# Linear memory in two blocks of 256 tokens, its decay factors made ahead and kept in DRAM, head outputs normed on ScalarE

## The chip, the core and the metric

One core of a Trainium2 chip runs the whole program. The time is the device time of one execution, in microseconds (us), as the median of several runs; beside it stands one profiled execution, whose own trace every duration below is taken from. The engines are TensorE (PE, with its weight loads PEld), VectorE (DVE), ScalarE (ACT), GpSimd (POOL) and SyncE (SP, which here only issues transfers). [...]

## What is computed

One layer of a streaming encoder on 512 prompt tokens and 64 sample tokens, D_MODEL = 1024: a feed-forward block, then a mixer of two branches (a linear memory with 4 heads of width 256, and a banded attention with 16 heads), then a second feed-forward block. The change touches the linear memory. For one head, with chunks of 64 tokens, the reference does

```
bcum = jnp.cumsum(lf, axis=-1)
dmat = jnp.where(causal, bcum[..., :, None] - bcum[..., None, :] + li[..., None, :], -jnp.inf)
m_t = jnp.maximum(inter, jnp.max(dmat, axis=-1))
s = jnp.einsum('bhtd,bhsd->bhts', q, k) * jnp.exp(dmat - m_t[..., None])
num = w_inter[..., None] * jnp.einsum('bhtd,bhde->bhte', q, C) + jnp.einsum('bhts,bhse->bhte', s, v)
den = w_inter * jnp.einsum('bhtd,bhd->bht', q, n) + jnp.sum(s, axis=-1)
h = num / jnp.maximum(jnp.abs(den), jnp.exp(-m_t))[..., None]
C_new = decay[..., None, None] * C + jnp.einsum('bhs,bhsd,bhse->bhde', w_s, k, v)
```

and then a layer norm of h over the head, a learned gain, a sigmoid gate from `ml_o`, and a projection. q and k come from a causal convolution of four taps with silu. The result does not depend on how the tokens are cut into chunks, so a kernel may choose its own.

## The kernel before

**Arithmetic.** Every matrix product is done in three float32r products: each operand x is split into a rounded half `hi` and the rest `lo = x - hi`, and `mm3` (line 138) issues hi*hi, hi*lo, lo*hi into one PSUM bank. A split costs one ACT instruction (the copy to `hi`) and one DVE subtraction (the `lo`), or for some weights a second ACT instruction and a transfer that adds (`add_lo`, line 222). `gemm` (line 381) makes a column tile of 128 outputs for all 576 tokens in two halves of 256 and 320 tokens, with 24 matmuls each.

**Order.** The order of PE is that of the Python program. `Order` (line 42) keeps an estimated clock `od.now`; `mm` (line 132) moves it forward by an estimate of each matmul. `later(dt, fn)` queues a function to be called dt nanoseconds of that clock later, between the steps of a `gemm`; so small products of one head lie inside the column tiles of the next. `od.bg` holds generators (`gate_rows`, `os_split`, `ht_split`) of which one step is taken at fixed distances. The order on ACT, DVE, POOL and SP is made by the tile scheduler, from priorities. PSUM has four banks with the tag "mm" and four with "aux"; `bank()` (line 123) hands out the latter.

**Gate rows.** `gate_rows` (line 1391) makes, for the four heads together, the running maximum `mrow` and rows of factors, and turns them into columns `tcol` (line 1363, 12 wide) and a split row tile `mr`.

**Attention and what follows it.** After the attention heads, a loop (line 1810) makes the gate columns 64 to 69 (`gemm` with `keep_cb`, line 1806) and `g58`; meanwhile `os_split` (line 1829) splits the eight attention outputs (names `o`, halves `os`), forms four sums of each pair in place on DVE, and splits these. Then `ap_pair` (line 1879) does the attention's projection two columns at a time in seven products of half size (`seven`, line 888) instead of eight; each product is 12 matmuls of 288 columns. Its first product takes the first splits of the outputs 4 to 7, the second those of 0 to 3, the third the second splits of 0 to 3, and the fourth the second splits of 4 to 7.

**The heads.** `ml_kq(h)` (line 1986) runs four column tiles (k in two halves, q in two halves), each followed by the convolution: ACT copies PSUM to `R`, DVE makes `U` in one and three instructions, ACT applies silu, ACT and DVE split. `turn5` (line 1973) transposes k and v into token order. `ml_decay` (line 2035) multiplies a row of `mr` by a selecting column to spread the running maximum over all partitions (`Mb`), and `decays` makes for the blocks b = 0 to 3 of 128 tokens the factors exp(a_s - M_t) for s in the block and all t from its start to 511 (widths 512, 384, 256, 128) and for the sample tokens (64 x 64); POOL blanks the part above the diagonal. `ml_early` (line 2074): `weights(b)` multiplies k and q of that shape (6 matmuls of width 512, 384, 256, 128 or 64), DVE multiplies by the factors, ACT and DVE split into `W`. `ml_late` (line 2113): `state(e)` sums the four prompt blocks into the new memory (12 matmuls) and the sample's block (3), `hidden(b)` sums over the blocks up to b (3 matmuls for each), ACT copies it to `hf`, DVE takes mean and variance; `norm` (line 2158) joins denominators and variance and does the subtraction and scaling of the five blocks on DVE; `back(e)` transposes to features and multiplies by gain and gate. The factors take exp, the convolution silu: an `order` table makes ACT do each head's exps together, with a table load (`ACT_TABLE_LOAD`) on either side.

Of the kernel before, what the change touches and what calls it, by code (L numbers as in the profile page):

```python
# [17 lines left out]
P = 128  # L18
NP_ = 512
# [67 lines left out]
def tile_layer(ctx: ExitStack, tc: tile.TileContext, ins, outs):  # L87
# [1275 lines left out]
    tcol = gp.tile([P, 5, 12], F32, name="tcol")  # L1363
# [18 lines left out]
    gdone = []  # L1382
    vf0, kf0, qf0 = (slot(F32, tp, t) for t in ("vf0", "kf0", "qf0"))
# [7 lines left out]
    def gate_rows():  # L1391
# [26 lines left out]
        for i, (a, b) in enumerate(((0, NP_), (NP_, T))):  # L1418
            ts(scol[:, 4 + i:5 + i], mrow[:, b - 1:b], -1.0, None, ALU.mult)
            yield act(rows[32:36, a:b], arow[:, a:b], AF.Exp, bias=scol[:, 4 + i:5 + i])  # L1420
# [9 lines left out]
        for b in range(5):  # L1430
            w = min(P, T - b * P)
            ps = bank()
            transpose(ps[:w, :P], rows[:, b * P:b * P + w], ident)
            yield DVE.tensor_copy(tcol[:w, b, :].rearrange("p (g h) -> p g h", h=4),
                                  ps[:w, :96].rearrange("p (g r) -> p g r", r=32)[:, :, 0:4])
# [370 lines left out]
    def keep_cb(hf, ps, j):  # L1806

        act(hs(sg[j], hf), ps, AF.Copy if j <= 3 else AF.Sigmoid)

    for j in range(KT):  # L1810
# [6 lines left out]
        if j == 3:  # L1817
# [3 lines left out]
            tstack.close()  # L1821
            ospool = tc.tile_pool(name="os", bufs=32, reuse_waits="tile")
# [6 lines left out]
            def os_split():  # L1829
# [29 lines left out]
                for s_ in sg[:4]:  # L1859
                    yield act(s_, s_, AF.Sigmoid)  # L1860
# [9 lines left out]
    def g58_cb(hf, ps):  # L1870
        act(hs(g58, hf), ps, AF.Sigmoid)
        if hf == 1:
            SP.dma_start(GD[2], g58)

    gemm(one(("in", 58)), H, [g58_cb])
    od.force(lambda: osq)
# [32 lines left out]
    ostack.close()  # L1909

# [41 lines left out]
    def conv_rest(ct, scale, room, tail=None):  # L1952
# [6 lines left out]
        with tc.issue_after(order["exp"].ins) if "exp" in order else nullcontext():  # L1959
            for a, b, u in ((0, NP_, 0), (NP_, T, NP_ + 3)):  # L1960
                order["silu"] = act(q[:, a:b], U[:, u:u + b - a], AF.Silu)
# [22 lines left out]
    hid, states, backs, order = [0], [0], [0], {}  # L1984

    def ml_kq(h):
# [19 lines left out]
        for e in range(2):  # L2006
# [9 lines left out]
            def v_turn(vf, sink):  # L2016

                if hid[0] < 5 * h:
                    later(300, lambda: v_turn(vf, sink))
                else:  # L2020
                    turn5(vf, sink)
# [13 lines left out]
    def ml_decay(h, st):  # L2035

        mb, mb2 = bank(), bank()
        pick = sel[:, h:h + 1].to_broadcast([P, P])
        mm(mb, pick, mr[:, :NP_], True, True)
        mm(mb2[:, 0:130], pick, mr[:, NP_:], True, True)  # L2040
        Mb = mp.tile([P, T], F32, tag="Mb", name=nm("Mb"))
        wdb = mp.tile([P, 66], F32, tag="wdb", name=nm("wdb"))
        with tc.high_priority(offset=120):
            act(Mb[:, :NP_], mb)
            act(Mb[:, NP_:], mb2[:, 0:64])
            act(wdb, mb2[:, 64:130])
# [8 lines left out]
        D = st["D"] = {}  # L2055

        def decays():

            for b in (4, 0, 1, 2, 3):
                s0 = b * P  # L2060
                n, w = (NP_ - s0, P) if b < 4 else (NS, NS)
                d = D[b] = mp.tile([P, n], F32, tag=f"D{b}", name=nm("D"))
                with tc.issue_after(order["silu"].ins):
                    order["exp"] = act(d[:w, :], Mb[:w, s0:s0 + n], AF.Exp, scale=-1.0, bias=tcol[:w, b, h:h + 1])

                POOL.affine_select(out=d[:w, 0:w], in_=d[:w, 0:w], pattern=[[1, w]], compare_op=ALU.is_ge, fill=0.0,
                                   base=0, channel_multiplier=-1)
            with tc.issue_after(order["exp"].ins):
                act(ch, c0v)
            tt(cl, c0v, f(ch), ALU.subtract)  # L2070

        later(6000, decays)

    def ml_early(h, st):
# [15 lines left out]
        def weights(b):  # L2090
            s0 = b * P
            n, w = (NP_ - s0, P) if b < 4 else (NS, NS)
            ps, d = bank(), D[b]
# [15 lines left out]
        for b in range(5):  # L2109

            later(10000 + 2100 * b if h == 3 else 11000 + 2600 * b, lambda b=b: weights(b))

    def ml_late(h, st):
        W, (c0, ch, cl), wdb, qs_ = st["W"], st["C"], st["wdb"], st["qs"]
        mv = mp.tile([P, 5, 2], F32, tag="mv", name=nm("mv"))
        dn = mp.tile([P, 5, 2], F32, tag="dn", name=nm("dn"))

        def state(e):
# [3 lines left out]
            for s in range(4):  # L2122
                mm3(ps[:, :258], kwh[:, s, ce], kwl[:, s, ce], vh[:, s, :], vl[:, s, :], s == 0, s == 3)
            cn = mp.tile([P, 258], F32, tag="cn", name=nm("cn"), bufs=2)
            with tc.high_priority(offset=100):
                act(cn, ps[:, :258])
            SP.dma_start(outs["pC"][h, :, e, :], cn)
            ps = bank()
            mm3(ps[:, :258], kwh[:, 4, ce], kwl[:, 4, ce], vh[:, 4, :], vl[:, 4, :], True, True)
            cn = mp.tile([P, 258], F32, tag="cs", name=nm("cs"), bufs=2)  # L2130
# [3 lines left out]
            states[0] += 1  # L2134

        def hidden(b):
# [13 lines left out]
            with tc.high_priority(offset=60):  # L2150
                act(hf_[:w, b, :], ps[:w, :258])
# [6 lines left out]
        def norm():  # L2158
# [11 lines left out]
            tt(rs, rs, r, ALU.mult)  # L2170
            for b in range(5):
                w = P if b < 4 else NS
                ts(hf_[:w, b, 0:256], hf_[:w, b, 0:256], mv[:w, b, 0:1], rs[:w, b:b + 1], ALU.subtract, ALU.mult)
# [19 lines left out]
        for e in range(2):  # L2193
            later(5500 + 1800 * e, lambda e=e: state(e))
        for b in range(5):
            later(16000 + 1800 * b if h == 3 else 19500 + 2200 * b, lambda b=b: hidden(b))
# [171 lines left out]
```

## Time and profile before

| | us |
|---|---|
| median of 3 runs (1545.62 to 1550.26) | 1546.3 |
| the profiled execution | 1547.03 |
| its span in the trace | 1544.8 |
| PE busy | 1528.6 |
| DVE busy | 1170.6 |
| ACT busy | 880.9 |
| POOL busy | 197.2 |

The profiled execution lies 0.7 us above the median, and 2.2 us of it lie outside the span. Stages in the span's time: first feed-forward and norm to about 400 us, the gate columns to about 560, attention to about 776, gate columns 64 to 69 and 58 from there to 802, the attention's projection to 847, the four heads of the linear memory to 1034, its projection, the output projection and the second feed-forward to the end.

How to read the rows: a timeline row gives start, duration, engine, line, operation, the written tile and the tiles it reads, their shape, a count, and in brackets how long the engine was idle before and what ended that. A row that groups instructions gives a count, the time in which at least one of them ran, and the mean duration. Matmuls overlap, so the time from one start to the next is the price of one, not its duration; instructions of ACT and DVE overlap by about 0.1 us when they follow each other.

### The profile page before, as it was taken

Reading aid. Unit: us, or ns where it says so; the run is one execution under the profiler, and the core shown is the slowest. Engines: PE = TensorE matmul, PEld = TensorE weight load, DVE = VectorE, ACT = ScalarE, POOL = GpSimd, SP = SyncE. Lnnn points to the kernel's source line nnn. Section 1 sums busy time; section 2 is a strip of 40 time slices with the busy share of each in tenths; the row PEclk is TensorE's granted clock in tenths of the full one; section 3 lists DMA queues with packets and bytes.
Section 4 is the critical chain, followed back from the end, with each engine's and each line's share of the span. In section 5 each row is a group of like instructions: output and inputs, shape, how many; then the busy total and the mean of one; then the engine's idle time right before and its main releaser. Section 6 shows DMA issues by size and latency. Waiting matters only on the chain.

```text
span 1544.8 us, 29439 instructions
## 1 busy us (share of the span) xinstructions
PE 1528.6 (99%) x11563; PEld 1513.4 (98%) x11563; DVE 1170.6 (76%) x2222; ACT 880.9 (57%) x1684; POOL 197.2 (13%) x370
## 2 busy tenths in 40 slices
PE   9999999999999999999999999999999999999998
PEld 9999999999999999999999999999999999999997
DVE  7877778776898767887677577775788888787765
ACT  7545446534666557777864877753456454557332
POOL 1000000100200015544200321102120000001000
PEclk9999999999999999999999999999999999999999
DMA  8322223524544449687544965542653223217333
GB/s 246 109 104 89 96 96 102 144 81 142 150 145 148 145 176 234 151 212 165 140 108 154 275 152 131 130 132 83 202 121 104 109 83 110 83 66 188 88 110 113
DMA packets 81075, 209.23 MB, mean 135 GB/s; under 512 B 9385, under 2 KB 23081, under 8 KB 80937
## 3 DMA queue, kind: packets, MB, share of 16 engines
q1 hardware_dynamic: 64936, 168.36, 32.2%
q0 software_dynamic: 14848, 37.30, 13.5%
q8 instruction: 90, 1.47, 0.4%
q10 hardware_dynamic: 1152, 1.70, 0.3%
q14 instruction: 49, 0.39, 0.1%
HBM read 170.89 MB, written 22.22 MB: 125 GB/s over the span
## 4 chain that ended last, share of the span: by engine, by line
PE 79%; DVE 9%; ACT 5%; DMA 3%; issue 3%; POOL 1%; SPq 0%; ACTq 0%; DVEq 0%; POOLq 0%
PE mm L133 67%; PE aux L133 11%; PE aux L143 1%; DVE wl L150 1%; ACT wh L147 1%; DMA s<-in_xT 1%; DVE s L150 1%; DVE sc L1608 1%; DVE s L153 1%; DVE o L150 1%; DVE U L153 1%; ACT sc L147 1%; DVE sc L157 1%; DMA wr<-in_w_in 1%; DVE kl L150 1%
## 5 line engine op out<-in xcount | busy, mean ns | idle before, releaser
L133 PE MATMUL mm<-s,wh 128*128 128x288 f32 (+2 forms) x3494 | 713.4, 298 | 1.0 <-DVE s L150 0.7
L133 PEld LDWEIGHTS mm<-s,wh 128*128 128x128 f32 x3494 | 558.7, 189 | 3.8 <-issue 0.9
L133 PE MATMUL mm<-s,wl 128*128 128x288 f32 (+2 forms) x1737 | 512.7, 295 | 0.0
L133 PEld LDWEIGHTS mm<-s,wl 128*128 128x128 f32 x1737 | 327.1, 188 | 0.2 <-DVE wl L150 0.2
L147 ACT ACTIVATE wh<-wr 128x1024 fp32r<-128x1024 f32 (+2 forms) x126 | 116.8, 935 | 108.3 <-PE mm L133 59.8
L133 PE MATMUL mm<-tx,wh 128*128 128x288 f32 x778 | 158.4, 296 | 0.0
L133 PEld LDWEIGHTS mm<-tx,wh 128*128 128x128 f32 x778 | 124.9, 188 | 0.0
L150 DVE TENSOR_TENSOR wl<-wr,wh 128x1024 fp32r<-128x1024 f32 (+2 forms) x87 | 90.8, 1053 | 36.6 <-ACT wh L147 36.5
L133 PE MATMUL mm<-tx,wl 128*128 128x288 f32 x383 | 113.0, 295 | 0.7 <-DVE wl L150 0.7
L976 ACT ACTIVATE wh<-wt 128x1024 fp32r<-128x1024 f32 x53 | 56.2, 1060 | 88.9 <-DVE wt L150 88.9
L150 DVE TENSOR_TENSOR wl<-wt,wh 128x1024 fp32r<-128x1024 f32 x53 | 64.8, 1222 | 52.6 <-ACT wh L976 52.6
L150 DVE TENSOR_TENSOR wl<-wu,wh 128x1024 fp32r<-128x1024 f32 x50 | 61.2, 1223 | 21.6 <-ACT wh L976 21.6
L223 POOL DMA_DIRECT2D s<-s x16 | 13.7, 855 | 495.0 <-ACT s L147 252.1
L133 PEld LDWEIGHTS mm<-tx,wl 128*128 128x128 f32 x383 | 72.0, 188 | 0.9 <-DVE wl L150 0.9
L147 ACT ACTIVATE h<-h 128x288 f32<-128x288 f32 x80 | 34.9, 437 | 65.2 <-DVE h L150 65.1
L976 ACT ACTIVATE wh<-wu 128x1024 fp32r<-128x1024 f32 x50 | 52.9, 1058 | 32.7 <-PE mm L133 32.5
L150 DVE TENSOR_TENSOR wl<-ws,wh 128x1024 fp32r<-128x1024 f32 x53 | 64.6, 1219 | 0.1
L150 DVE TENSOR_TENSOR ws<-wu 128x1024 f32<-128x1024 f32 x53 | 64.5, 1216 | 0.0
L133 PE MATMUL mm<-h,wh 128*128 128x256 f32 (+2 forms) x296 | 60.2, 294 | 0.0
L976 ACT ACTIVATE ah<-wu 128x512 fp32r<-128x512 f32 x53 | 33.4, 631 | 44.4 <-PE mm L133 41.3
L976 ACT ACTIVATE wh<-ws 128x1024 fp32r<-128x1024 f32 x53 | 55.8, 1052 | 0.7 <-PE mm L133 0.4
L147 ACT ACTIVATE sc<-sc,mx 128x128 f32<-128x128 f32 (+4 forms) x72 | 40.3, 560 | 25.1 <-DVE mx L1608 24.7
(420 smaller groups left out, 3609.0 us busy)
## 6 DMA issues: line engine op xcount, KB each, us to landing
wu<-in_w_gu SPq DMA_DIRECT2D x80, 512.0 KB, 4.4
wr<-in_w_in SPq DMA_DIRECT2D x46, 512.0 KB, 4.1
wl<-in_w_in POOLq DMA_DIRECT2D x38, 512.0 KB, 6.5
wr<-in_w_dn SPq DMA_DIRECT2D x34, 512.0 KB, 3.5
wu<-in_w_in SPq DMA_DIRECT2D x26, 512.0 KB, 4.7
wr<-in_w_dn SPq DMA_DIRECT2D x18, 384.0 KB, 3.5
s<-s POOLq DMA_DIRECT2D x16, 288.0 KB, 3.8
wr<-in_w_ap SPq DMA_DIRECT2D x8, 512.0 KB, 3.5
```

Source lines behind the costliest of these rows:

```text
L133: PE.matmul(out, lhsT, rhs, start=start, stop=stop, **kw)
L143: PE.transpose(out, in_, idn)
L147: return ACT.activation(out, in_, func, **kw)
L150: return (eng or DVE).tensor_tensor(out, a, b, op=op)
L153: return DVE.scalar_tensor_tensor(out=out, in0=a, scalar=s, in1=b, op0=op0, op1=op1)
L157: return (eng or DVE).tensor_scalar(out=out, in0=a, scalar1=s1, scalar2=s2, op0=op0, **kw)
L223: return POOL.dma_start(lo, src, accum_op=ALU.add)
L976: self.last = ACT.activation(hi, src, AF.Copy)
L1608: DVE.tensor_tensor_reduce(out=out, in0=ps, in1=g, op0=ALU.add, op1=ALU.min, scale=-1.0, scalar=3e38, accum_out=acc)
```

## The change

**Two blocks of 256 tokens (NC = 256).** The prompt's 512 tokens are cut in two. Within each half all is as before, so `weights(b)` has the widths 256, 128, 256, 128 and 64. `first(e)` sums blocks 0 and 1 into the memory after the first half (`cf`, split into `cfh`, `cfl`); `carried(b)` multiplies the q of blocks 2 and 3 by it, ACT scales it by a per-token factor (new columns of `tcol`, made by one more exp in `gate_rows`), and `hidden(2)` and `hidden(3)` add it on DVE instead of being copied by ACT. `second(e)` sums blocks 2 and 3 and joins them with `cf` by a factor `g`; `sample(e)` is the sample's part of what was `state`.

**Decay factors ahead.** `decay_rows(h)` makes all factors of head h and the factor g; the four heads are queued 300 + 2600 h ns after the attention's last use of its pool, in the loop of the gate columns. They go to DRAM (`DK`), and `ml_decay` fetches them into one tile with two buffers. What stays in `ml_decay` is one matmul of 66 columns. Sigmoids between the attention and the projection are held until the fourth head's exps are done (`issue_after(dexp[3].ins)`); the gate columns 64 to 69 are first copied and later passed through sigmoid.

**Norm on ScalarE.** The last step of `norm` is an `Identity` activation with scale and bias per token.

**Distances.** The `later` distances of weights, state, hidden and carried are changed, and two turns of v are kept 2500 ns apart.

Its core:

```diff
-    tcol = gp.tile([P, 5, 12], F32, name="tcol")
+    tcol = gp.tile([P, 5, 16], F32, name="tcol")
...
+    NC = NP_ // 2
...
+        yield act(rows[96:100, NC:NP_], mrow[:, NC:NP_], AF.Exp, bias=mrow[:, NC - 1:NC], scale=-1.0)
+        for i, (a, b) in enumerate(((0, NC), (NC, NP_), (NP_, T))):
...
-        act(hs(sg[j], hf), ps, AF.Copy if j <= 3 else AF.Sigmoid)
+        act(hs(sg[j], hf), ps)
...
+    def decay_rows(h):
+        mb, mb2 = bank(), bank()
+        pick = sel[:, h:h + 1].to_broadcast([P, P])
+        mm(mb, pick, mr[:, :NP_], True, True)
+        mm(mb2[:, 0:NS], pick, mr[:, NP_:T], True, True)
+        Mb = dkp.tile([P, T], F32, tag="Mb", name=nm("Mb"))
+        with tc.high_priority(offset=120):
+            act(Mb[:, :NP_], mb)
+            act(Mb[:, NP_:], mb2[:, 0:NS])
+        D = dkp.tile([P, DW], F32, tag="D", name=nm("D"), bufs=2)
+        for b in range(5):
+            s0 = b * P
+            n, w = (NC - s0 % NC, P) if b < 4 else (NS, NS)
+            d = D[:w, DB[b]:DB[b] + n]
+            act(d, Mb[:w, s0:s0 + n], AF.Exp, scale=-1.0, bias=tcol[:w, b, h:h + 1])
+            POOL.affine_select(out=d[:, 0:w], in_=d[:, 0:w], pattern=[[1, w]], compare_op=ALU.is_ge, fill=0.0,
+                               base=0, channel_multiplier=-1)
+        dexp.append(act(D[:, DG:DG + 1], Mb[:, NP_ - 1:NP_], AF.Exp, scale=-1.0, bias=Mb[:, NC - 1:NC]))
+        SP.dma_start(DK[h][:, 0:DG + 1], D[:, 0:DG + 1])
+        SP.dma_start(DK[h][0:NS, DB[4]:], D[0:NS, DB[4]:])
...
+            for h in range(4):
+                later(300 + 2600 * h, lambda h=h: decay_rows(h))
...
+                    with tc.issue_after(dexp[3].ins):
+                        yield act(s_, s_, AF.Sigmoid)
...
+    for s in sg[4:6]:
+        with tc.issue_after(dexp[3].ins):
+            act(s, s, AF.Sigmoid)
...
-            for b in (4, 0, 1, 2, 3):
-                s0 = b * P
-                n, w = (NP_ - s0, P) if b < 4 else (NS, NS)
-                d = D[b] = mp.tile([P, n], F32, tag=f"D{b}", name=nm("D"))
-                with tc.issue_after(order["silu"].ins):
-                    order["exp"] = act(d[:w, :], Mb[:w, s0:s0 + n], AF.Exp, scale=-1.0, bias=tcol[:w, b, h:h + 1])
+        D = st["D"] = mp.tile([P, DW], F32, tag="D", name=nm("D"), bufs=2)
+        SP.dma_start(D[:, 0:DG + 1], DK[h][:, 0:DG + 1])
+        SP.dma_start(D[0:NS, DB[4]:], DK[h][0:NS, DB[4]:])
...
-            for s in range(4):
-                mm3(ps[:, :258], kwh[:, s, ce], kwl[:, s, ce], vh[:, s, :], vl[:, s, :], s == 0, s == 3)
+            for s in range(2):
+                mm3(ps[:, :258], kwh[:, s, ce], kwl[:, s, ce], vh[:, s, :], vl[:, s, :], s == 0, s == 1)
+            with tc.high_priority(offset=100):
+                act(cf[:, e, :], ps[:, :258])
+            act(cfh[:, e, :], cf[:, e, :])
+            tt(cfl[:, e, :], cf[:, e, :], f(cfh[:, e, :]), ALU.subtract)
...
+                stt(cn, cf[:, e, :], st["g"][:, 0:1], ps[:, :258], ALU.mult, ALU.add)
...
+        def carried(b):
+            ps = bank()
+            for e in range(2):
+                qh, ql = (x[:, b * P:(b + 1) * P] for x in st["q"][e])
+                mm3(ps[:, :258], qh, ql, cfh[:, e, :], cfl[:, e, :], e == 0, e == 1)
+            with tc.high_priority(offset=100):
+                act(hc_[:, b - 2, :], ps[:, :258], scale=tcol[:, b, 12 + h:13 + h])
...
-                          vh[:, s, :], vl[:, s, :]) for s in range(b + 1)]
+                          vh[:, s, :], vl[:, s, :]) for s in range(b // 2 * 2, b + 1)]
...
+                if b in (2, 3):
+                    tt(hf_[:, b, :], ps[:, :258], hc_[:, b - 2, :], ALU.add)
...
-                ts(hf_[:w, b, 0:256], hf_[:w, b, 0:256], mv[:w, b, 0:1], rs[:w, b:b + 1], ALU.subtract, ALU.mult)
+                act(hf_[:w, b, 0:256], hf_[:w, b, 0:256], AF.Identity, bias=dn[:w, b, 1:2], scale=rs[:w, b:b + 1])
...
-            later(16000 + 1800 * b if h == 3 else 19500 + 2200 * b, lambda b=b: hidden(b))
+            later(17000 + 1800 * b if h == 3 else 20500 + 2200 * b, lambda b=b: hidden(b))
```

More of the change, by code (lines that the diff above doesn't have):

```diff
@@ L1958, in conv_rest @@
         hi, lo = room(), room()
-        with tc.issue_after(order["exp"].ins) if "exp" in order else nullcontext():
-            for a, b, u in ((0, NP_, 0), (NP_, T, NP_ + 3)):
-                order["silu"] = act(q[:, a:b], U[:, u:u + b - a], AF.Silu)
+        for a, b, u in ((0, NP_, 0), (NP_, T, NP_ + 3)):
+            act(q[:, a:b], U[:, u:u + b - a], AF.Silu)
         @hot(300)
@@ L2193, in ml_late @@
         for e in range(2):
-            later(5500 + 1800 * e, lambda e=e: state(e))
+            later(4500 + 1300 * e, lambda e=e: first(e))
+            later(7000 + 2400 * e, lambda e=e: second(e))
+            later(8200 + 2400 * e, lambda e=e: sample(e))
+        for b in (2, 3):
+            later(14000 + 2000 * (b - 2) if h == 3 else 16300 + 2600 * (b - 2), lambda b=b: carried(b))
         for b in range(5):
-            later(16000 + 1800 * b if h == 3 else 19500 + 2200 * b, lambda b=b: hidden(b))
+            later(17000 + 1800 * b if h == 3 else 20500 + 2200 * b, lambda b=b: hidden(b))
         later(25500 if h == 3 else 31000, norm)
```

66 lines of the change are left out of this document (38 added, 28 removed).

## The prediction, made before the changed kernel was run

> **What bounds the kernel now.** The page comes first: the span, and each engine's busy time in it.
>
> ```profile
> span 1544.8 us, 29439 instructions
> PE 1528.6 (99%) x11563; PEld 1513.4 (98%) x11563; DVE 1170.6 (76%) x2222; ACT 880.9 (57%) x1684; POOL 197.2 (13%) x370
> ```
>
> PE has work for all but 16 us of the span. An average can hide a stage with another limit, so the table by stage comes next: the stretch in which the decay factors are now to be made (783 to 802 us), and the heads (860 to 1020 us). Its columns are length, then busy time and count of PE, PEld, DVE, ACT and POOL, then granted clock, DMA share and GB/s.
>
> ```profile
> 783.00:802.00 19.00, 19.00 (x145) 19.00 (x144) 19.00 (x37) 12.96 (x24) 0.00 (x0) 1.00 0.22 56
> 860.00:900.00 40.00, 39.84 (x306) 39.21 (x305) 27.18 (x55) 33.88 (x77) 8.69 (x22) 1.00 0.94 255
> 900.00:940.00 40.00, 40.00 (x310) 39.48 (x308) 30.25 (x80) 29.74 (x68) 7.94 (x22) 1.00 0.55 134
> 980.00:1020.00 40.00, 40.00 (x315) 39.55 (x314) 29.99 (x78) 29.59 (x69) 6.66 (x18) 1.00 0.44 107
> ```
>
> PE is full in all of them at a granted clock of 1.00; ACT has 10 of 40 us free in a head, and 6 of 19 between 783 and 802. So the time changes by two things only: PE work that disappears, and waits of PE that appear or go. PE's waits for tiles in the attention and the heads (560 to 1050 us) add up to 4 us; the change touches two of the rows (total, times, longest), the second for the spread maximum `Mb`:
>
> ```profile
> PE aux L143 <- DVE ptl L150: 2.1, 4, 1.0
> ...
> PE aux L143 <- ACT Mb L147: 0.2, 1, 0.2
> ```
>
> **PE work that goes.** Grouped by shape, the products `weights(b)`, six matmuls per block and head:
>
> ```profile
> L133 PE MATMUL aux<-qk,s 128*128 128x512 f32 x24 | 6.2, 396 | 0.0
> L133 PE MATMUL aux<-qk,s 128*128 128x384 f32 x24 | 4.8, 336 | 0.0
> L133 PE MATMUL aux<-qk,s 128*128 128x256 f32 x24 | 3.4, 277 | 0.0
> L133 PE MATMUL aux<-qk,s 128*128 128x128 f32 x24 | 3.1, 266 | 0.0
> ```
>
> After the change the widths are 256, 128, 256, 128. The 512 become 256: 6.2 - 3.4 = 2.8 us. The 384 become 128: 4.8 - 3.1 = 1.7 us. Together **-4.5 us**, all of it on the path.
>
> The matmuls of 258 columns do not become fewer, which is what one would hope from two blocks. Per head, before: state 2 x (12 + 3) = 30, hidden 3 x (1 + 2 + 3 + 4) = 30 and 9 for the sample, 69. After: first 2 x 6, second 2 x 6, sample 2 x 3, carried 2 x 6, hidden 3 x (1 + 2 + 1 + 2) = 18 and 9: 69. What the shorter sums save, the carried memory costs. That is **0**.
>
> The spreading of the maximum moves to the earlier loop, as a pair per head; a third small one (66 columns) stays.
>
> ```profile
> 937.79 0.51 PE L133 MATMUL aux<-mr,sel 128*128 128x512 f32 x2
> 938.14 0.45 PE L133 MATMUL mm<-s,wh 128*128 128x256 f32 x2
> ```
>
> The pair takes 938.14 - 937.79 = 0.35 us in each head. The new pair (512 and 64 columns) is narrower by 66, and those 66 remain: taken as 0; at most the remaining one costs 4 x 0.1 us, an estimate from the 3.1 / 24 = 0.13 us of a 128-column one.
>
> **Waits that go.** The 0.2 us above, and one of the four in the attention:
>
> ```profile
> 755.51 1.05 ACT L147 ACTIVATE wh<-wr 128x1024 fp32r<-128x1024 f32 x1
> 756.58 1.28 ACT L147 ACT_TABLE_LOAD   x1
> 757.87 0.69 ACT L147 ACTIVATE s<-s 128x576 f32<-128x576 f32 x1
> 770.11 0.66 PE L143 MATMUL aux<-ident,sc 128*128 128x128 f32 x4 [0.38 <-DVE ptl L150]
> ```
>
> Sigmoids that the scheduler put between the softmax's exps cost two table loads each time, at 757 and again ahead of 770, where PE then waits 0.38 us for the late split. Held behind the fourth head's exps, they leave this place. What is late next there is another split of the same pair; both waits together **-0.6 us** (0 to -0.6).
>
> **The decay factors in the loop of gate columns.** This is the largest unknown. Everything held and added queues on ACT, in this order after the weight split at 782.95, and the last attention splits `os` queue behind it. Prices, by the step from one start to the next or the mean less 0.1 us of overlap:
>
> ```profile
> 782.95 1.06 ACT L147 ACTIVATE wh<-wr 128x1024 fp32r<-128x1024 f32 x1 [0.79 <-PE mm L133]
> 783.92 0.42 ACT L147 ACTIVATE s<-mm 128x320 f32<-128x320 f32 x1
> 784.24 0.68 ACT L147 ACTIVATE os<-o 128x576 fp32r<-128x576 f32 x1
> 798.44 0.63 ACT L147 ACTIVATE wh<-s 128x512 fp32r<-128x512 f32 x1
> 798.98 0.37 ACT L147 ACTIVATE s<-mm 128x256 f32<-128x256 f32 x1
> 799.24 2.40 ACT L147 ACTIVATE os<-o 128x576 fp32r<-128x576 f32 x4
> L147 ACT ACT_TABLE_LOAD x10 | 12.8, 1283 | 0.2
> L147 ACT ACTIVATE D<-Mb,tcol 128x256 f32<-128x256 f32 x4 | 2.0, 504 | 0.0
> L147 ACT ACTIVATE D<-Mb,tcol 128x128 f32<-128x128 f32 x4 | 1.6, 400 | 0.0
> L147 ACT ACTIVATE D<-Mb,tcol 64x64 f32<-64x64 f32 x4 | 1.4, 342 | 0.0
> L147 ACT ACTIVATE Mb<-aux 128x512 f32<-128x512 f32 x4 | 2.4, 599 | 0.0
> L147 ACT ACTIVATE Mb<-aux 128x64 f32<-128x64 f32 x4 | 0.9, 234 | 0.0
> ```
>
> Per head the exps cost 0.41 + 0.31 + 0.41 + 0.31 + 0.25 and 0.19 for the one-column g (an estimate: 342 ns less the 0.9 ns per column that separates 64 and 128), 1.87 us; the two copies 0.50 + 0.13 = 0.63. Four heads: 10.0. Beside them stand two weight splits of 1024 (0.97 each), five of 512 (0.54), seven PSUM copies (three 0.26, four 0.32), two copies of projection results (0.31), eleven `os` (0.60), five sigmoids (0.60) and one table load (1.28): 1.9 + 2.7 + 2.1 + 0.6 + 6.6 + 3.0 + 1.3 = 18.2. The sum, 28.2 us, ends at 811.2, and the DVE half of the last split at about 811.9 (a step of 0.7).
>
> ```profile
> 800.25 2.78 DVE L150 TENSOR_TENSOR os<-o,os 128x576 fp32r<-128x576 f32 x4
> 807.06 0.41 ACT L147 ACTIVATE o<-mm 128x288 f32<-128x288 f32 x1 [0.67 <-PE mm L133]
> 808.70 0.41 ACT L147 ACTIVATE o<-mm 128x288 f32<-128x288 f32 x1 [1.23 <-PE mm L133]
> ```
>
> Before, that split was done at 803.0, and its reader, the fourth product of the first pair of projection columns, ran from 806.9 to 808.5, between the ends that release these two copies. With four pairs of spreading matmuls ahead (4 x 0.29 = 1.15 us) it runs from 808.05 to 809.65, and its last quarter needs the last `os` at 809.25. So PE waits 811.9 - 809.25 = **+2.6 us**. The ends: 0.5 if the eleven splits keep DVE's and ACT's gaps better filled than I assume or some exps precede 782.95; 5 if POOL's masking (20 of them) or the second buffer of `D`, which the third head reuses once the first store has landed, holds an exp up by 2 us. I take the sum of the queue. The stores themselves stand in SP's queue ahead of the gate's and the projection's weight loads; the DMA share there is 0.22, so I price them at nothing.
>
> [...]
>
> **The last head's tail.** Its normalisation has no next head to hide in. `T0` is the end of the sample's `hidden`, 1026.46.
>
> ```profile
> 1026.72 0.36 ACT L147 ACTIVATE hf<-aux 64x258 f32<-64x258 f32 x1
> 1027.67 0.16 DVE L153 SCALAR_TENSOR_TENSOR dn<-hf,tcol 128x5 f32<-128x5 f32 x1
> 1030.37 0.17 DVE L150 TENSOR_TENSOR mrs<-mrs,dn 128x5 f32<-128x5 f32 x1 [1.31 <-POOL mrs L579]
> 1030.57 1.70 DVE L157 TENSOR_SCALAR hf<-hf,mv,mrs 128x256 f32<-128x256 f32 x5
> 1026.62 6.40 PE mm L133 x48
> 1033.02 1.09 PE aux L143 x10
> ```
>
> Before, 48 matmuls (6.40 us) cover the chain: copy, denominators, variance, POOL's root, scaling, ready at 1032.3 for transposes at 1033.0. In the order of instructions after, only 6 of 256 columns and 24 of 320 stand between: 6 x 0.12 + 24 x 0.147 = 4.3 us. The chain starts 0.3 after T0; in before it took from 1026.72 to 1030.54 with a weight's split in the way at DVE; without that I take 3.2 us to `rs`. Then comes the new DVE step (0.2) and five Identity on ACT instead of five on DVE (0.34 each). An Identity with two operands per token was never run here; the nearest rows are exp with one (504 ns for 256 columns) and a copy with none,
>
> ```profile
> L147 ACT ACTIVATE W<-D 128x256 fp32r<-128x256 f32 x4 | 1.7, 419 | 3.4 <-DVE D L150 3.4
> ```
>
> 504 - 419 = 85 ns for an operand, so 0.59 with two, a step of 0.49. The fifth is done at T0 + 0.3 + 3.2 + 0.2 + 2.5 = T0 + 6.2, and the transposes, which take 1.09, end at about 6.9, since those of early blocks run ahead of it. Unobstructed they would end at 4.3 + 1.1 = 5.4. So **+1.5 us** (0.5 to 2.5, by 0.2 per Identity and by whether the weight split still cuts in).
>
> **Heads 0 to 2.** ACT loses two or three table loads a head (10 in the stage, 12.8 us) and the exps; the scaling by Identity costs it 2.5. Nothing there was waited for, so this gains nothing. DVE takes over two PSUM reads and gives back five scalings. POOL loses its masks. The work of a head on the three engines stays below its 40 us. A tight place appears: `hidden(2)` follows `hidden(0)` into the same bank within some 2.5 us, and the copy that empties it can stand on ACT behind a `W` split. I take **+0.5** over the four heads (0 to 4, one missed copy of 1 us in each).
>
> **Sum.** -4.5 - 0.6 + 2.6 + 1.5 + 0.5 = -0.5 us against 1547.03 of the profiled execution: 1546.5. That execution lies 0.7 above the median, so the forecast for the median is **1545.8**.
>
> **The rivals.**
> 1. *The new waits are hidden* (faster): ACT takes exps in gaps before 783 and the tail is covered. For it: 6 of 19 us of ACT are idle there; against it, the sum of 28 us. Only -4.5 - 0.6 is left: 1546.3 - 5.1 = 1541.2.
> 2. *Every head waits for a PSUM bank* (slower): `hidden(2)` cannot start until ACT has copied `hidden(0)`; likewise `second` behind `first`, whose two copies stand in ACT's queue. It decides from about 1.4 us of lateness per head, where it eats the 5.1 gained; at 2 us a head the 0.5 becomes 8: 1553.3. For it: four banks with shorter distances and more users (first, second, sample and carried have a bank each). Against it: ACT gets freer by some 3 us per head.
> 3. *The narrower products are no cheaper*, since the weight load bounds them: the change then does not do what it says. The 4.5 is missing: 1550.3. The four rows by shape speak against it.
> [...]
>
> **How the numbers follow.** Forecast 0.55, rivals 0.20, 0.15, 0.04, 0.06. A measurement of this kernel tells about 0.3% from no change, 4.6 us: faster is below 1541.7, slower above 1550.9. Rival 1 is faster in nine cases of ten and the forecast in a fiftieth: 0.19. Rival 2 gives most of the 0.16 for slower. The rest is 0.65. The range goes down to rival 1 less the 0.7 by which the lowest run lies under the median, 1540.5, and up to the forecast with the wait at its upper end (+2.4), the tail at its (+1.0) and half of the upper end of the heads (+2), 1551.2; rival 2 at its own price and the lower edge of rival 1 stay out, under 0.2.
>
> **What would show it.** In the profile after: `weights` of 512 and 384 columns gone, with the 256 and 128 groups doubled at the same mean; 69 matmuls of 258 columns a head; PE idle of 2 to 3 us near 810, released by DVE `os`; one of 1 to 2 us near 1032 before the transposes of `hf`, released by ACT; no wait of PE for a bank above 0.5 us in a head. The prediction is wrong if PE is idle in the heads by more than 2 us, or nowhere.

## The result, and the profile after

The change makes the kernel slower. Six runs of it have a median of 1555.93 us (1554.80 to 1557.77), six of the kernel before 1547.49 us (1545.62 to 1550.26): ratio 1.0054, 95% interval 1.0041 to 1.0067. The forecast was 1545.8 us with a range of 1540.5 to 1551.2. The profiled execution took 1555.86 us.

The page of the kernel after gives span and busy times:

```profile
span 1553.9 us, 29490 instructions
PE 1531.6 (99%) x11567; PEld 1514.0 (97%) x11567; DVE 1171.1 (75%) x2231; ACT 880.2 (57%) x1710; POOL 201.0 (13%) x370
```

The span is 9.1 us longer and PE is busy for 3.0 us more, though the narrower products are there. Grouped by shape, in the heads:

```profile
L133 PE MATMUL aux<-qk,s 128*128 128x256 f32 x48 | 7.0, 281 | 0.0
L133 PE MATMUL aux<-qk,s 128*128 128x128 f32 x48 | 6.2, 266 | 0.0
```

The four groups of before (17.5 us) have become two (13.2 us). So work was saved, and more than that was lost. Where it was lost is shown by the waits of PE in the kernel after (total, times, longest):

```profile
PE aux L143 <- DVE kwl L153: 3.6, 2, 2.7
...
PE aux L143 <- ACT hf L147: 1.3, 8, 0.2
...
PE mm L133 <- DVE os L150: 0.9, 2, 0.7
PE mm L133 <- ACT o L147: 0.6, 2, 0.5
...
PE mm L133 <- ACT os L147: 0.5, 1, 0.5
```

None of the first, second, third and fifth stood in the list of before. Two are at the places that the prediction named (`os` near 811 us, `hf` in the tail). The first, and largest, is at a place that it did not name.

The table by stage of the kernel after (length, busy times and counts, granted clock, DMA share, GB/s); of its columns the first, PE's busy time, and the granted clock matter here:

```profile
760.00:776.00 16.00, 16.00 (x129) 15.66 (x129) 8.79 (x28) 10.36 (x27) 0.86 (x1) 1.00 0.49 101
783.00:802.00 19.00, 19.00 (x143) 18.82 (x142) 13.85 (x26) 17.82 (x47) 8.96 (x20) 1.00 0.38 121
808.00:812.00 4.00, 2.72 (x17) 2.05 (x15) 3.67 (x6) 4.00 (x8) 0.00 (x0) 1.00 0.67 220
814.00:816.00 2.00, 2.00 (x10) 2.00 (x10) 0.42 (x2) 0.41 (x1) 0.00 (x0) 0.50 0.00 0
880.00:884.00 4.00, 1.16 (x8) 0.93 (x9) 3.44 (x9) 2.93 (x9) 1.16 (x3) 1.00 1.05 406
886.00:888.00 2.00, 2.00 (x11) 1.96 (x10) 0.83 (x3) 2.00 (x5) 0.24 (x1) 0.50 1.06 251
```

Between 783 and 802 us ACT is busy for 17.82 us instead of 12.96, as the sum of its queue said. PE is short of work twice, at 808 to 812 and at 880 to 884 us, and both times its clock is granted at 0.50 soon after: "busy" for 2.00 of 2.00 us, it issues 10 or 11 matmuls there, where 129 in 16 us, the first row, is 16 in 2 us. Here each wait is paid twice.

To place the loss exactly I matched the column tiles of the two traces: the start of the first matmul of a tile in the timeline of PE, after minus before. The tile that starts at 771.63 us before starts at 771.40, 0.24 earlier; at 802.10 it is 1.09 later, at 847.41 5.80, at 885.50 10.01, and at 1040.35 (output projection) 9.40 later. The growth over each stretch, for this kernel and the experiments below, in us:

| kernel | 771 to 802: gate columns | 802 to 847: projection | 847 to 885: first head begins | 885 to 1040: rest of the heads | sum |
|---|---|---|---|---|---|
| after | +1.3 | +4.7 | +4.2 | -0.6 | +9.6 |
| e1, ch late | +1.3 | +3.1 | -1.1 | +0.1 | +3.4 |
| e2, sigmoids late | +1.3 | +2.2 | +2.7 | -0.6 | +5.6 |
| e3, norm on VectorE | +1.3 | +3.8 | +3.3 | -3.3 | +5.2 |
| e4, all three | +1.3 | +3.1 | -1.3 | -3.5 | -0.4 |
| e5, factors in the heads | 0.0 | +0.3 | -0.9 | +3.1 | +2.4 |
| e6, norm alone on before | 0.0 | +0.4 | 0.0 | +0.3 | +0.6 |
| e8, factors in the projection | 0.0 | +7.9 | -1.3 | -2.2 | +4.4 |
| e9, stores from POOL | 0.0 | +4.1 | +0.3 | -3.6 | +0.8 |
| e10, two and two | +0.7 | +0.8 | +0.7 | -3.6 | -1.4 |

An undisturbed stretch repeats within 0.4 us (e5 and e6 in the projection, where their programs are those of before). A disturbed one does not: up to 847 us the kernel after, e1 and e3 have the same program, and their projections lose 4.7, 3.1 and 3.8 us. The start at 771 us lies up to 1.7 us from that of before, so the growth, and not the time of a profiled run, is compared. Each row is one execution; those traced of e1 and e8 are the shortest of their five, 3.2 and 5.3 us under the medians, so their rows show less than the median loses.

The largest loss, 847 to 885 us, is read from ScalarE's timeline of the kernel after and two rows of PE:

```profile
870.25 1.06 ACT L147 ACTIVATE wl<-wh 128x1024 fp32r<-128x1024 f32 x1
876.47 0.64 ACT L147 ACTIVATE ch<-c 128x516 fp32r<-128x516 f32 x1 [5.16 <-DMA c<-in_C]
877.01 0.36 ACT L147 ACTIVATE R<-mm 128x256 f32<-128x256 f32 x1
```

```profile
880.12 0.55 PE L143 MATMUL aux<-ident,qf 128*128 128x128 f32 x3 [0.85 <-DVE kwl L153]
883.50 0.30 PE L143 MATMUL aux<-ident,qf 128*64 128x128 f32 x1 [2.72 <-DVE kwl L153]
```

The copy of the old memory to `ch`, which PE first reads at 918.4 us, stands at the head of ScalarE's queue and waits 5.16 us for its transfer; ScalarE did nothing else in that time. Behind it stand the copy of the second column tile (877.01) and the copies to `kwh`; VectorE's `kwl` follows these, and PE cannot write the next transposes into the bank until `kwl` has read it. VectorE stands still for 4.56 us too, since its own half of this copy, `cl`, waits for `ch`; which of the two queues holds PE up longer is not separated here. The transfer itself was as slow before: from issue to landing it took 12.9 us in the first head after (the chain of the kernel after) and 12.5 before (the view of the tile `c`, 855 to 870 us):

```profile
863.51 12.93 DMA c<-in_C
```

```profile
857.60 0.53 SPq L2051 DMA_DIRECT2D c<-in_C  x1
DMA to landing us min/median/max: 12.5/12.5/12.5
```

It is issued at 863.51 instead of 857.60, 5.9 us later, about the lateness of the whole program at that point. What differs is the place of the copy. Before, it was held behind the head's exps, with these rows of ScalarE:

```profile
873.18 1.31 ACT L147 ACTIVATE D<-Mb,tcol 128x384 f32<-128x384 f32 x3
874.38 0.64 ACT L147 ACTIVATE ch<-c 128x516 fp32r<-128x516 f32 x1
```

It ran 16.8 us after the issue, with nothing in brackets: no wait. The change took the exps and their ordering out of the heads, and with them the cover of this copy. These are the lines of the change that did it:

```diff
-            with tc.issue_after(order["exp"].ins):
-                act(ch, c0v)
...
+        def carry_parts():
+            act(ch, c0v)
...
-        later(6000, decays)
+        later(6000, carry_parts)
```

### The profile page after: what moved, and what is told of

Read it like the earlier page. It is cut to its first block, busy times and chain, and to the rows that moved or that the text cites. A ratio compares the mean times of both kernels' runs of the same rounds, so it can differ in the third digit from the quotient of the medians.

```text
span 1553.9 us, 29490 instructions
## 1 busy us (share of the span) xinstructions
PE 1531.6 (99%) x11567; PEld 1514.0 (97%) x11567; DVE 1171.1 (75%) x2231; ACT 880.2 (57%) x1710; POOL 201.0 (13%) x370
## 4 chain that ended last, share of the span: by engine, by line
PE 78%; DVE 9%; ACT 4%; DMA 4%; issue 3%; POOL 1%; SPq 0%; ACTq 0%; DVEq 0%; POOLq 0%
PE mm L133 65%; PE aux L133 11%; PE aux L143 1%; DVE wl L150 1%; DMA c<-in_C 1%; DMA wr<-in_w_in 1%; ACT wh L147 1%; DVE s L150 1%; DVE sc L1610 1%; DVE s L153 1%; DVE o L150 1%; DVE sc L157 1%; ACT hf L147 1%; DMA s<-in_xT 1%; DVE kl L150 1%
## 5 line engine op out<-in xcount | busy, mean ns | idle before, releaser
L976 ACT ACTIVATE wh<-wt 128x1024 fp32r<-128x1024 f32 x53 | 56.2, 1060 | 89.8 <-DVE wt L150 89.3
```

The source lines that it names most:

```text
L976: self.last = ACT.activation(hi, src, AF.Copy)
```

## The experiments

Times are medians, each beside the kernel before on the same chip: 1547.74 us for e1, e2, e3 and e5, 1546.72 for e4, e6 and e8, 1547.07 for e9 and e10.

### e1: the copy to ch behind the third tile's silu

```diff
-            act(q[:, a:b], U[:, u:u + b - a], AF.Silu)
+            silu[:] = [act(q[:, a:b], U[:, u:u + b - a], AF.Silu)]
...
-            act(ch, c0v)
+            with tc.issue_after(silu[0].ins):
+                act(ch, c0v)
...
-        later(6000, carry_parts)
+        later(12000, carry_parts)
```

> The changed kernel with one edit: the copy of a head's old memory to ch (ScalarE) may be issued only behind the silu of the third column tile of that head, so that it no longer stands ahead of the second tile's copies while its transfer is under way. Theory A (ch at the head of ScalarE's queue waits 5.16 us for its transfer and holds up the copies behind it, so TensorE waits 3.6 us near 880 and then runs at a lower clock): the matched column tiles behind 885 us are 4 to 5 us earlier, the clock between 880 and 900 is 1.00, time 1551.4 (1550.5 to 1552.3). Theory B (the new transfers of the decay factors delay all loads at the start of the heads, and whichever comes last holds TensorE up): another load takes the place of ch, time 1554 to 1556.

Measured: 1552.88 us, ratio 1.0039 (1.0026 to 1.0052). The stretch 847 to 885 us went from +4.2 to -1.1, by 5.3 us, and the kernel has no wait for `kwl`. Its table by stage, where the copy now lies (880.63, no wait):

```profile
812.00:816.00 4.00, 3.90 (x29) 3.90 (x30) 3.59 (x8) 1.84 (x4) 0.00 (x0) 1.00 0.02 4
860.00:880.00 20.00, 20.00 (x155) 19.97 (x154) 12.79 (x24) 14.08 (x32) 4.78 (x11) 1.00 1.05 319
880.00:900.00 20.00, 20.00 (x158) 19.84 (x157) 15.62 (x36) 15.66 (x40) 3.56 (x10) 1.00 0.97 278
```

PE is full and its clock 1.00. Theory A holds; the transfers of the factors are still there with a DMA share of 1.05, so theory B falls. The median lies 0.6 above the expected interval and its ratio's interval still overlaps that of the change: the trace decides here, not the time. Against the kernel before, the medians lose 5.1 us here and 8.4 in the kernel after, so by them the edit is worth 3.3 us. The first row shows something else: in this execution the wait near 811 us is the same, but the clock stays at 1.00 behind it, and the projection loses 3.1 instead of 4.7 us.

### e2: the sigmoids behind the last attention split

```diff
-                    act(hi, r)
+                    last = act(hi, r)
...
-                for s_ in sg[:4]:
-                    with tc.issue_after(dexp[3].ins):
-                        yield act(s_, s_, AF.Sigmoid)
+                dexp.append(last)
...
+    for s in sg[:6] + [g58]:
+        with tc.issue_after(dexp[-1].ins):
+            act(s, s, AF.Sigmoid)
```

> The changed kernel with one edit: all seven sigmoids of the gates, with their table load, are issued behind the last split of the attention outputs; gate column 58 is copied first. Theory A (the queue on ScalarE between 783 and 812 us is too long by what was held into it): without five sigmoids (3.0) and a table load (1.3) the last split ends 4.3 earlier, TensorE's waits of 1.4 us for os near 811 go, and with them the lower clock of 812 to 816; of the 4.7 us that the stretch from 802 to 847 us lost, some 4 come back and the stall in the first head stays: time 1552 (1551 to 1553). Theory B (the stall in the first head is a consequence of this lateness): both go, time 1547. Theory C (the sigmoids are now late for the projection's products with the gates): TensorE waits for those, time 1554 or more.

Measured: 1553.84 us, ratio 1.0043 (1.0031 to 1.0055). The last split now starts at 808.95 instead of 810.92, 2.0 us earlier (2.5 against the matched tile at 802 us, which starts 0.5 later here) and not 4.3:

```profile
804.55 0.69 ACT L147 ACTIVATE os<-o 128x576 fp32r<-128x576 f32 x1 [0.99 <-DVE o L153]
...
808.95 0.68 ACT L147 ACTIVATE os<-o 128x576 fp32r<-128x576 f32 x1
```

With the sigmoids gone from the queue, ScalarE waits for VectorE's sums instead (0.99 us in the first row). The projection still loses 2.2 us. With the sigmoids in their old place it lost 4.7, 3.1 and 3.8 (the kernel after, e1, e3), so the edit is worth 0.9 to 2.5 us there and not 4. The wait for `kwl` in the first head is still there, 2.9 us in all, though the program arrives 2.0 us less late: theory B falls. e8, below, starts the heads later still, with the copy to `ch` held back as in e1, and its waits for `kwl` are 0.5 us where those of the kernel after are 3.6. No wait for the gates is in the list, as theory C would have it. Theory A has the place and the direction right, with a smaller amount, and the time lies above its range.

### e3: subtraction and scaling on VectorE again

```diff
-            stt(v, mv[:, :, 0], -1.0, rs, ALU.mult, ALU.mult)
...
-                act(hf_[:w, b, 0:256], hf_[:w, b, 0:256], AF.Identity, bias=dn[:w, b, 1:2], scale=rs[:w, b:b + 1])
+                ts(hf_[:w, b, 0:256], hf_[:w, b, 0:256], mv[:w, b, 0:1], rs[:w, b:b + 1], ALU.subtract, ALU.mult)
```

> The changed kernel with one edit: the subtraction and scaling of the five blocks is again one VectorE instruction each, and the added product of mean and scale is gone. Theory A (five Identity at a step of 0.49 us end the last head's chain, against 0.34 on VectorE, and the same happens in the first head at 930 us): the tail's transposes end 0.9 us earlier and the eight waits for hf (1.3 us, about 2.5 us with slowed transposes) go: time 1554 (1553.3 to 1554.9). Theory B (the chain through POOL's root sets the end, and VectorE's scaling waits behind a weight's split): no change, 1555.5 to 1556.3.

Measured: 1553.61 us, ratio 1.0039 (1.0027 to 1.0051). The rest of the heads went from -0.6 to -3.3, by 2.7 us, and the eight waits for `hf` are gone: theory A. 1.3 us of it is the tail (from the tile at 1003.52 to that at 1033.86 before: +1.6 in the kernel after, +0.3 here), 1.0 is the first head's transposes at 930 us (from the tile at 919.99 to that at 927.66: +1.1 and +0.1).

### e6: the norm on ScalarE alone, in the kernel before

```diff
+            stt(v, mv[:, :, 0], -1.0, rs, ALU.mult, ALU.mult)
...
-                ts(hf_[:w, b, 0:256], hf_[:w, b, 0:256], mv[:w, b, 0:1], rs[:w, b:b + 1], ALU.subtract, ALU.mult)
+                act(hf_[:w, b, 0:256], hf_[:w, b, 0:256], AF.Identity, bias=dn[:w, b, 1:2], scale=rs[:w, b:b + 1])
```

> The kernel before with one part of the change alone: subtraction and scaling by Identity on ScalarE. Theory A (the tail's loss in the changed kernel comes from its 30 covering matmuls where 48 stood before, and the Identity's step of 0.49 us only counts because of that): with the 48 in place the fifth block is ready some 0.3 us after the transposes begin, and the matched column tile behind them moves by 0 to 0.6 us. Theory B (Identity costs the same anywhere): 1.5 us, with waits of the transposes for each block.

One execution, 1546.37 us. The tail's tile (1033.86) moved by +0.17 against the tile ahead of it, and no wait for `hf` of 0.2 us or more stands in the list of waits. The five scalings take what they take in the kernel after (2.57 us), with 48 matmuls as cover. ScalarE and PE in this kernel:

```profile
1030.31 2.57 ACT L147 ACTIVATE hf<-hf,dn,mrs 128x256 f32<-128x256 f32 x5 [3.12 <-DVE dn L153]
```

```profile
1032.38 1.43 PE L143 MATMUL aux<-ident,hf 128*128 128x128 f32 x10
```

The slower step costs only where the cover was shortened: theory A.

### e5: two blocks, but the factors in the heads again

The factors, the order of exps and silu, and the sigmoids are those of before; blocks, Identity and distances those of after. The core, in `ml_decay`:

```diff
-        D = st["D"] = mp.tile([P, DW], F32, tag="D", name=nm("D"), bufs=2)
-        SP.dma_start(D[:, 0:DG + 1], DK[h][:, 0:DG + 1])
+            for b in (4, 0, 1, 2, 3):
+                n, w = (NC - s0 % NC, P) if b < 4 else (NS, NS)
+                with tc.issue_after(order["silu"].ins):
+                    order["exp"] = act(d[:w, :], Mb[:w, s0:s0 + n], AF.Exp, scale=-1.0, bias=tcol[:w, b, h:h + 1])
+            with tc.issue_after(order["exp"].ins):
+                order["exp"] = act(g, Mb[:, NP_ - 1:NP_], AF.Exp, scale=-1.0, bias=Mb[:, NC - 1:NC])
```

> Two blocks of 256 tokens and the Identity norm as in the changed kernel, but the decay factors are made in each head by its own exps again, with the order of exps and silu and without the transfers; the gates' sigmoids stand where they stood before the change. Theory A (nearly all the loss comes from making the factors ahead: the queue in the gate loop and the uncovered copy of the old memory): the narrower products' 4.5 us are kept, the tail and the first head's transposes cost 1.5 each: time 1545.5 (1543.5 to 1547.5), TensorE's clock 1.00 throughout 780 to 1040 us. Theory B (the two-block arithmetic with its additional PSUM tiles and copies is what costs): 1550 or more, with waits of TensorE for PSUM tiles spread over all heads.

Measured: 1550.86 us, ratio 1.0024 (1.0015 to 1.0034): outside theory A's range. The time is one that theory B allows, but its waits are not there. The gate loop, the projection and the start of the first head are undisturbed (0.0, +0.3, -0.9), as theory A says, but the first head now has another wait, and the clock falls behind it:

```profile
PE aux L133 <- DVE D L150: 1.9, 1, 1.9
```

```profile
900.00:904.00 4.00, 4.00 (x25) 4.00 (x24) 2.87 (x6) 3.39 (x9) 1.17 (x3) 0.61 0.42 137
```

From the tile at 895.30 to that at 900.59 this loses 4.0 us. So two blocks are not free without the factors made ahead either. Waits for PSUM tiles spread over all heads (theory B) are not in the list: this is one place, in one head. Why the factors meet the products in just this head I did not test.

### e4: e1, e2 and e3 together

> The changed kernel with the three edits before together: ch behind the third tile's silu, sigmoids behind the last split of the attention outputs, scaling on VectorE. Theory A (the three losses are separate): counted on matched column tiles against the kernel before, the attention gives -0.7, the four added pairs of spreading matmuls +1.3, what is left of the wait in the projection +2.2, the first head's stall 0, the head stage as a whole -1.1 (as with ch alone) less 2.3 (as with VectorE alone): -0.6 in all, so the time of the kernel before less half a microsecond, ratio 1.000 (0.999 to 1.001). Theory B (taking one wait away uncovers another): ratio 1.002 or more.

Measured: 1546.17 us, ratio 0.9997 (0.9988 to 1.0006). Expected 1.000: theory A. The stall in the first head and the waits for `hf` are gone (no wait of PE stands in the list from 850 to 1060 us), and the three edits together bring the kernel from 1.0054 to the time of before. The head stage gains 4.8 us, near the 4.3 of the narrower products and some 1 us (an estimate from the 0.35 us of a pair) of the spreading matmuls that moved out. The gate loop and the projection take 4.4 of it. The projection loses 3.1 us and not the 2.2 of e2 and of the expectation, as much as e1 without the later sigmoids: what that edit brings in this kernel is not shown.

### e8: e4 with the factors made in the projection

```diff
-            for h in range(4):
-                later(300 + 2600 * h, lambda h=h: decay_rows(h))
...
+    for h in range(4):
+        later(2500 + 9500 * h, lambda h=h: decay_rows(h))
     for j in range(0, KT, 2):
         ap_pair(j)
```

> As the kernel with the three edits together, and the decay factors of the four heads are made 9500 ns apart in the attention's projection (where ScalarE is busy 4 of 10 us) instead of 2600 ns apart in the loop of the gate columns (8.9 of 10). Theory A (the factors cost TensorE only their eight matmuls where ScalarE has room): no wait of TensorE for os at 811 us, the stretch from 802 to 847 us longer by 1.3 us against the kernel before and the loop unchanged; 2 to 2.5 us faster than the kernel before, ratio 0.9985 (0.9975 to 0.9995). Theory B (the exps come between the projection's PSUM copies, and TensorE waits for banks there): ratio 1.000 or more.

Measured: 1556.98 us, ratio 1.0068 (1.0054 to 1.0081), a miss, and as slow as the change. In the traced execution (1551.68 us) the wait for `os` is gone, the loop undisturbed, but the projection loses 7.9 us; where the 5.3 us more of the median are lost, no trace shows. PE's waits between 800 and 862 us, and SP's queue in the middle of them:

```profile
PE mm L133 <- DVE o L150: 3.5, 3, 1.7
PE mm L133 <- ACT wh L147: 1.0, 1, 1.0
```

```profile
832.17 0.45 SPq L1838 DMA_DIRECT2D dk<-D  x1
832.72 0.54 SPq L1837 DMA_DIRECT2D dk<-D  x1
833.35 0.38 SPq L297 DMA_DIRECT2D wr<-in_w_ap  x1
```

The stores of the factors come after the exps, the last of which ended at 831.04 + 0.28 = 831.32 us, and the projection's next weights stand behind them on SP. That gave e9.

### e9: the stores from GpSimd's queue

```diff
-        SP.dma_start(DK[h][:, 0:DG + 1], D[:, 0:DG + 1])
-        SP.dma_start(DK[h][0:NS, DB[4]:], D[0:NS, DB[4]:])
+        POOL.dma_start(DK[h][:, 0:DG + 1], D[:, 0:DG + 1])
+        POOL.dma_start(DK[h][0:NS, DB[4]:], D[0:NS, DB[4]:])
```

> The kernel with the decay factors made in the projection, with one edit: the factors are stored to DRAM from GpSimd's queue instead of SyncE's. Theory A (the stores stood in SyncE's queue ahead of the projection's weight loads, each waiting for its exps and masks, so the loads of 833 and 847 us were issued 5 us late): TensorE's waits of 3.5 us for o and 1.0 for wh between 820 and 860 us go, the stretch from 802 to 847 us is 1.3 to 2.5 us longer than before the change instead of 7.9, ratio 0.9990 (0.998 to 1.000). Theory B (the exps between the projection's PSUM copies hold the copies up): the waits stay, ratio 1.004 or more.

Measured: 1548.47 us, ratio 1.0012 (1.0004 to 1.0021), between the two expectations. The weights that were issued at 833.35 are now issued at

```profile
830.46 3.03 SPq L297 DMA_DIRECT2D wr<-in_w_ap  x2
```

and the waits for `o` fell from 3.5 to 0.4 us; the projection loses 4.1 instead of 7.9. The queue was the larger part. The wait for `wh` stayed at 1.0 us, so theory A did not have all of it; that this part is the exps between the copies (theory B) was not tested.

### e10: two heads' factors in the loop, two in the projection

```diff
-            for h in range(4):
-                later(300 + 2600 * h, lambda h=h: decay_rows(h))
+            for h in range(2):
+                later(300 + 5700 * h, lambda h=h: decay_rows(h))
...
+    for h in (2, 3):
+        later(12000 * (h - 1), lambda h=h: decay_rows(h))
     for j in range(0, KT, 2):
```

> With the three edits and the stores from GpSimd's queue, two heads' factors are made in the gate loop (300 and 6000 ns) and two in the projection (12 and 24 us into it). Theory A (the wait in front of the fourth product comes from the length of ScalarE's queue, now 24 - 5 = 19 us from 783, done by 803): no wait of TensorE for os; against the kernel before, attention -0.7, gate loop +0.7, projection +0.7 to 1.5, head stage -4.8 as in the kernel with three edits: -3.3 to -4.1 us, ratio 0.9977 (0.9970 to 0.9988). Theory B (any work added to ScalarE around the projection's first products is paid by TensorE): ratio 0.9995 or more.

Measured: 1544.23 us, ratio 0.9983 (0.9974 to 0.9992): faster than both kernels, by 2.8 us against before. Its table by stage:

```profile
783.00:802.00 19.00, 19.00 (x144) 18.95 (x144) 18.90 (x35) 16.32 (x39) 16.66 (x14) 1.00 0.25 67
802.00:820.00 18.00, 18.00 (x137) 17.96 (x137) 11.29 (x20) 14.75 (x27) 0.83 (x3) 1.00 0.47 164
820.00:840.00 20.00, 19.93 (x149) 19.52 (x147) 17.26 (x30) 11.53 (x28) 6.39 (x12) 1.00 0.51 172
```

PE loses 0.07 us in these 57 us. The ratio lies within theory A's interval and the wait for `os` is gone. The matched tiles give less than it said: the head stage gains 2.9 us and not 4.8, since PE waits for `kwl` in the first head (1.2 us at 876 us). The copy to `ch` is not its cause: it runs only at 879.38, without a wait. e10 differs from e4 in two things, where the factors are made and the queue of their stores; no run separates them.

## Why the prediction was wrong, step by step

- **PE work that goes**: -4.5 predicted, 17.5 - 13.2 = 4.3 measured. Right. So is the count of 258-column matmuls: the rows by shape of the heads add up to 276, four times 69.
- **Waits that go**: -0.6 predicted; the tiles at 771 us start 0.66 earlier against those of the early attention, and PE is busy for 16.00 of 16.00 us from 760 to 776. Right.
- **The queue in the gate loop**: its length was nearly right. The last split ended on ScalarE at 810.92 + 0.69 = 811.61; the sum said 811.2. The table load took the 1.28 us that the sum has for it, from 800.15 to 801.43, and its sigmoid started at 801.44. ScalarE also waited 1.09 us at 792.49 for the first store of `D` to land, which the prediction had named for its upper end and left out of the sum. The price was mis-sized: 2.6 predicted, +4.7 measured over the projection, 3.1 in e1 and 3.8 in e3.

```profile
810.92 0.69 ACT L147 ACTIVATE os<-o 128x576 fp32r<-128x576 f32 x1
```

```profile
811.58 0.40 PE L133 MATMUL mm<-os,wh 128*128 128x288 f32 x1 [0.66 <-DVE os L150]
...
814.15 0.69 PE L133 MATMUL mm<-os,wh 128*128 128x288 f32 x2
814.63 0.45 PE L133 MATMUL mm<-os,wl 128*128 128x288 f32 x1
```

The waits themselves add up to 0.47 + 0.49 + 0.66 + 0.22 = 1.8 us. What was left out is the clock behind them: three matmuls from 814.15 to the next three at 814.87 take 0.72 us, where 0.39 is normal, for some 3.4 us, or 1.6 us of loss; e1, whose clock did not fall there, lost 3.1 instead of 4.7. Of the remaining 1.3 us some 0.7 is an estimate from these rows: a matmul's row is 0.30 us long where its step is 0.13, so each of four waits costs 0.17 more than its idle time. The rest is open. A fall of the clock stood nowhere in the prediction.
- **The tail**: transposes ending at T0 + 6.9 predicted. T0 is 1036.31 in the kernel after, and the next tile starts at 1043.28. Right, for the reason given: e6 shows that the same Identity costs 0.2 us with the longer cover.

```profile
1040.03 2.57 ACT L147 ACTIVATE hf<-hf,dn,mrs 128x256 f32<-128x256 f32 x5 [2.43 <-DVE dn L153]
```

- **Heads 0 to 2**: this is the step that failed. "Nothing there was waited for, so this gains nothing" looked at ScalarE's load and at PE's waits, and priced +0.5. The load did fall. But the exps were not only load: the copy to `ch` was ordered behind them, and that order kept a slow transfer (12.93 us) off the head of ScalarE's queue. The diff shows the removed `issue_after` in so many words, but the prediction did not ask what had stood behind it. Its price in the traced executions is 5.3 us (e1), of which the waits are 3.6 and the halved clock behind them most of the rest. In e2, whose clock did not fall there, the same stretch grew by 2.7 where e1's shrank by 1.1, so there it is 3.8. The prediction's own sign of being wrong, PE idle in the heads by more than 2 us, came true. The Identity took another 1 us in the first head, which the prediction allowed only in the tail.
- **Rivals**: the second (a PSUM bank in every head) was right in sign, but not in mechanism: no wait for a bank of `hidden` or `second` stands in the list; the wait for `kwl` is one for a bank, but in one head only and behind a transfer. The first and third fall with the rows above.

Summed: -0.7 + 1.3 + 4.7 + 4.2 - 0.6 = +8.9 on the trace (8.8 between the profiled executions), against -0.5 predicted.

## What to carry to other kernels

When a change takes work off an engine, list what was ordered behind that work and when the inputs of each such instruction land; one that is now reached early can hold up what stands behind it, as `ch` did for 5.16 us here, however much free time the engine's load shows. Work that is made ahead should be spread over stages by the length of the engine's queue up to the next deadline (here: 28 us up to 809 us, too long by 3; in e10 the last split was done by 801.3 us, and PE did not wait for it), and its stores should not stand in a queue ahead of weights. Moving it to the emptiest stage is not enough: e8 had ScalarE's room and lost as much as the change itself.

## What the runs showed of the hardware

PE's clock fell to half behind the same short waits in one execution and not in another. In the kernel after, the clock is 0.50 from 812.95 to 816.37 and from 884.63 to 888.04 us, 3.41 us each time, after stretches in which PE was busy for 2.72 and 1.16 of 4 us; in e1 it stays at 1.00 after 2.61 of 4. Up to there both programs are the same on PE and wait in the same places (the longest waits are 0.49 and 0.66 us in both), so the same wait costs 1.6 us more in one execution and not in another. Over whole executions the mean granted clock was 0.995 to 0.997 in the six runs of the kernel after and 0.998 to 0.999 in the eleven of e4, whose stall in the first head is gone.

The two falls of the kernel after begin 71.68 us apart. In the 3.41 us that end where the first begins, PE waits for 1.37 of the 1.96 us that it waits near 811 us; in e1 two stretches of that length, one after the other, hold 0.57 and 0.92 of its 1.88 us:

```profile
809.54:812.95 3.41, 2.04 (x9) 1.36 (x10) 3.21 (x5) 2.64 (x6) 0.00 (x0) 1.00 0.49 169
```

```profile
806.71:810.12 3.41, 2.84 (x18) 2.37 (x18) 2.73 (x4) 3.41 (x7) 0.00 (x0) 1.00 0.85 263
810.12:813.53 3.41, 2.49 (x14) 2.05 (x15) 3.26 (x6) 2.12 (x4) 0.00 (x0) 1.00 0.22 80
```

From 808 to 812 us, though, PE is idle for 1.28 us in the kernel after and for 1.39 in e1. The idle time does not decide alone: in e2 a stretch of 3.41 us with 1.07 us of it (626.39 to 629.80) is followed by a fall, and one with 1.87 (878.97 to 882.38, the stall in the first head) is not. What else counts is open.
